# Time mixing: the place of the modulation sums and of the gate's product in the slots

## The chip, the cores and the metric

The kernel runs on one core of one Trainium2 chip. The metric is the device time of one launch in microseconds (us), as the median of several runs.

## The reference

One sequence of 256 tokens with 2048 features goes through two layers. The first is RWKV-7 time mixing with a squared-ReLU MLP, the second chunked band attention with such an MLP. The change lies in the first layer's time mixing. Ahead of everything stand the adaLN modulations, vectors that are products of the condition `c` with large matrices:

```python
mod = c @ w_ada[layer] + b_ada[layer]                 # 2048 x 12288 per layer
sh1, sc1, gt1, sh2, sc2, gt2 = jnp.split(mod, 6, axis=-1)
h = modulate(rms_norm(x, g_mix[layer]), sh1, sc1)
...
r, k, v = xr @ w_r, xk @ w_k, xv @ w_v                # time mixing
g = jax.nn.sigmoid(xg @ g1) @ g2                      # the gate
def step(S, inp):                                     # per head of 64, over 256 tokens
    sa = jnp.einsum('bhvk,bhk->bhv', S, -kk_t)
    S = S * w_t[:, :, None, :] + sa[..., None] * (kk_t * a_t)[:, :, None, :] + v_t[..., None] * k_t[:, :, None, :]
    y = jnp.einsum('bhvk,bhk->bhv', S, r_t)
...                                                   # group norm of y, bonus term
y = y.reshape(B, T, D) * g
return y @ w_o
```

## The kernel before

All activations are kept transposed, with 128 features on the partitions and 256 tokens along the free axis. Matrices are read as float32, split into a high and a low part (ScalarE casts the high part `wH`, L424; VectorE subtracts, `wL`, L427) and multiplied in three passes (L447 to L449, the "projection").

**Slots.** Time mixing treats the 2048 features as 16 pairs of heads (class `Pair`). Each pair is cut into 36 steps: 8 early ones, 12 that invert a triangular matrix, and 16 late ones, which run the recurrence over four chunks, normalise and multiply by the gate. A loop over slots in `layer_a` advances every live pair by one step; a new pair starts every 8 slots, so four or five pairs are live at once. In slot s, pair j stands at step s - 8(j + 1). Within a slot the steps go in the order of a key: inversions first, then late steps (the oldest pair first), then early steps. The step that sums squares over partitions (the last but two) has the key raised by 2 and so comes last. Behind these small steps stand the slot's parts of the dense projections `k` and `r` of the next pair (after slot 128 parts of the output projection). `tc.issue_after(last)` keeps TensorE (PE) in this order; the order on the other engines is set by the scheduler, from the data that each instruction needs.

**Gate's product.** A pair's last step multiplies the gate's low-rank factor `tg` by its weights `lg` on PE (L369) into a PSUM buffer `ms`, and VectorE multiplies the result into `v` (L371). There are two `ms` buffers, and they serve all small steps: the inversion's last product leaves one of them only when ScalarE has copied it out as `uf` (L292).

**Modulation sums.** In six of eight slots, after the projection, `self.ada()` takes one tile of a modulation matrix and VectorE adds it, weighted with `c`, into one accumulator (`acc`, L503 for the first of 16 tiles, L505 for the others). After the 16th tile the accumulator has to be summed over partitions: `ada_sum` issues 32 narrow matmuls against a column of ones (L527) into an `ms` buffer and adds the bias on VectorE (L531). `ada_sum` is a generator, and `self.fin(n)` advances it:

```python
        if kt == KT - 1:
            self.fins = self.ada_sum(self.acc, self.mods[key], half, self.ada_src(*key)[1])
            if not self.lazy:
                self.fin(HK)
```

`lazy` is False throughout this kernel, so the matmuls follow the 16th tile's accumulation at once. There are six such sums in time mixing. The next tile of a new sum calls `fin` too, ahead of writing the accumulator.

Other names in the rows: `iv`, `tt`, `xs`, `u`, `al` belong to the inversion (L264 is VectorE's transpose `tt`, L281 and L276 are ScalarE's copies `xs`); `lt`, `g`, `sa`, `zs`, `kr`, `vp`, `mk` to the recurrence (L104, L348 for `zs`); L191 to L202 are the early steps' VectorE work, L173 to L185 their scan and ScalarE functions.

Of the kernel before, what the change touches and what calls it, by code (L numbers as in the profile page):

```python
# [30 lines left out]
HK = 8  # L31
# [343 lines left out]
class Body:  # L375
# [332 lines left out]
    def layer_a(self, st, sp):  # L708
        nc, tc, d = self.nc, self.tc, self.d
# [7 lines left out]
        with ExitStack() as s1:  # L717
# [19 lines left out]
            sums = pb.tile([P, 2, KT], F32, name="sums01")  # L737
# [117 lines left out]
            for n in range(KT):  # L855
# [12 lines left out]
                first, last = n == 0, n == KT - 1  # L868
# [45 lines left out]
        with ExitStack() as s1:  # L914
            pw = self.pw = s1.enter_context(tc.tile_pool(name="pw", bufs=1, reuse_waits="tile"))
            pp = self.pp = sp.enter_context(tc.tile_pool(name="ps_b", bufs=1, space=bass.MemoryType.PSUM,
                                                         reuse_waits="tile"))
            self.psm = lambda: pp.tile([P, 512], F32, tag="ms", bufs=2, name="ms")
            self.bones = pw.tile([P, P], F32R, name="bones")
            nc.scalar.copy(self.bones, self.cst("bones"))  # L920
            e01 = [pw.tile([P, 4, C + 1], F32, name=f"e01_{i}") for i in range(2)]
            self.uf = [pw.tile([P, 4, C], F32, name=f"uf_{i}") for i in range(2)]
            for e, u in zip(e01, self.uf):
                nc.vector.memset(e[:, :, 0:1], 1.0)
                nc.gpsimd.memset(u, 0.0)

            s1.enter_context(self.ada_room(3))
            self.ada_left = self.ADA_A
            pairs = [Pair(self, j, v[:, j, :], tw, ta, tg, e01[j % 2]) for j in range(NPAIR)]

            def proj_steps(pr):
                for dst, hl in (("k", xk), ("r", xr)):
                    ps = pp.tile([P, 2 * T], F32, tag="pj", bufs=1, name="pj")[:, :T]
                    for kt in range(KT):
                        if kt % HK == 0:
                            w = [self.w_made.popleft()] * (KT // HK)
                        self.proj(ps, w, lambda kt: hl[:, kt, :, 0:T], (kt, kt + 1))
                        if dst == "r" and kt == 1:
                            pr.lw = pw.tile([P, 2, P], F32, tag="lw", bufs=1, name="lw")
                            nc.sync.dma_start(out=pr.lw, in_=d["lora2"][pr.j, :, 0:2])  # L940
                        if kt % 2 == 1:
                            if kt == KT - 1:
                                t = pw.tile([P, T], F32, tag=dst, bufs=2, name=dst)
                                nc.scalar.copy(t, ps)  # L944
                                setattr(pr, dst, t)
                            yield

            def out_steps():

                for n in range(8):  # L950
                    self.split(self.y_hl, n, v[:, n, :])
                sums, todo = self.o_ps, [(n, 0, HK) for n in range(8)] + [(n, HK, KT - 2) for n in range(4)]
                for n, lo, hi in todo:
                    if n % 2 == 0 and lo == 0:
                        if n != 6:
                            tag, k = {0: ("pj", 1), 2: ("iv", 1), 4: ("gr", 2)}[n]
                            ps = pp.tile([P, k, 2 * T], F32, tag=tag, bufs=1, name="o")
                            sums += [ps[:, i].rearrange("p (i t) -> p i t", i=2) for i in range(k)]
                    if lo == HK and n == 0:
                        assert all(p.done for p in pairs[:KT - 2])  # L960
                        for j in range(HK, KT - 2):
                            self.split(self.y_hl, j, v[:, j, :])
                    w = self.weight_part(d["w_o"][n], lo, hi)
                    for kt in range(lo, hi, 2):
                        self.proj(sums[n // 2][:, n % 2, :], w, lambda kt: self.y_hl[:, kt, :, 0:T],
                                  (kt, kt + 2), n % 2 == 0, False)
                        yield

            self.o_ps = []
            S, OUTS = self.SLOTS, 44  # L970
            inverts = range(Pair.EARLY, Pair.EARLY + Pair.INVERT)
            outs, done, n_out = None, 0, 0
            for slot in range(S * NPAIR + Pair.STEPS):
                live = []
                for j, pr in enumerate(pairs):
                    at = slot - S * (j + 1)
                    if 0 <= at < Pair.STEPS:
                        if at == 0:
                            pr.gen = pr.steps()
                        sums = at == Pair.STEPS - 3  # L980
                        live.append((0 if at in inverts else 1 + (at < Pair.EARLY) + 2 * sums, -at, pr))
                        pr.done = at == Pair.STEPS - 1
                last = self.last_pe()
                for _, _, pr in sorted(live, key=lambda x: x[:2]):
                    with tc.issue_after(last):
                        next(pr.gen)
                    last = self.last_pe()
                if slot < S * NPAIR:
                    if slot % S == 0:
                        dense = proj_steps(pairs[slot // S])  # L990
                    todo = 16 // S
                else:
                    if outs is None:
                        self.y_hl = self.new_hl()
                        outs = dense = out_steps()
                    todo = OUTS * (slot + 1 - S * NPAIR) // Pair.STEPS - n_out
                    n_out += todo
                with tc.issue_after(last):
                    for _ in range(todo):
                        next(dense, None)  # L1000
                if slot == 2 * S - 4:
                    self.ada_fill()
                with self.behind():
                    if slot % S in (1, 3, 6, 7):
                        self.w_make()
                    if slot >= 2 * S and slot % S in (0, 1, 2, 4, 6, 7):
                        self.ada()
            self.ada_drain(3)
            self.ada_left = -1
            self.fin(HK)  # L1010
        return v

    def out_proj(self, pp, wname, hl, gate, g, sc, sh, begun=()):
# [310 lines left out]
```

## Time and profile before

| | |
|---|---|
| median of 3 runs | 2648.93 us (2644.81 to 2649.68) |
| the profiled execution | 2651.01 us, of which the span is 2649.2 us |
| PE busy | 2558.2 us, 97% of the span |
| mean granted clock of TensorE | 0.987 |
| time mixing's slots | about 217 to 700 us of the span |

The span reaches from the first to the last instruction of one profiled execution; its own time is 1.8 us more. Rows of a timeline give start, duration, engine, line, operation, output<-inputs, shapes and count, and in brackets how long the engine sat idle before and what released it. PEld is the load of TensorE's weights; a granted clock of 1.00 is full speed.

### The profile page before, as it was taken

Reading aid. Unit: us, or ns where it says so; the run is one execution under the profiler, and the core shown is the slowest. Engines: PE = TensorE matmul, PEld = TensorE weight load, DVE = VectorE, ACT = ScalarE, POOL = GpSimd, SP = SyncE. Lnnn points to the kernel's source line nnn. Section 1 sums busy time; section 2 is a strip of 40 time slices with the busy share of each in tenths; the row PEclk is TensorE's granted clock in tenths of the full one; section 3 lists DMA queues with packets and bytes.
Section 4 is the critical chain, followed back from the end, with each engine's and each line's share of the span. In section 5 each row is a group of like instructions: output and inputs, shape, how many; then the busy total and the mean of one; then the engine's idle time right before and its main releaser. Section 6 shows DMA issues by size and latency. Waiting matters only on the chain.

```text
span 2649.2 us, 58856 instructions
## 1 busy us (share of the span) xinstructions
PE 2558.2 (97%) x23980; PEld 2236.9 (84%) x23980; DVE 2084.7 (79%) x3022; ACT 1372.3 (52%) x2532; POOL 215.4 (8%) x338
## 2 busy tenths in 40 slices
PE   7998999999999999999999999999999999999997
PEld 4788888887899888888888998887898888888886
DVE  6887888888889888888888898899897555555555
ACT  3346566565455355354365554565564464453554
POOL 1002323232100000000001000000100000000002
PEclk9999999998999999999999999999999999999999
DMA  9975666565778889889898679887766555555553
GB/s 351 322 260 189 203 206 204 191 218 173 255 236 300 326 324 328 326 320 341 326 329 288 230 255 326 305 288 259 259 219 235 186 190 187 188 190 188 187 189 121
DMA packets 207664, 663.17 MB, mean 250 GB/s; under 512 B 21409, under 2 KB 55073, under 8 KB 207393
## 3 DMA queue, kind: packets, MB, share of 16 engines
q1 hardware_dynamic: 205328, 656.89, 72.2%
q8 instruction: 188, 3.08, 0.5%
q10 hardware_dynamic: 2064, 2.53, 0.3%
q14 instruction: 84, 0.68, 0.1%
HBM read 657.23 MB, written 2.10 MB: 249 GB/s over the span
## 4 chain that ended last, share of the span: by engine, by line
PE 72%; DVE 1%; DMA 0%; issue 0%; ACT 0%; DVEq 0%; SPq 0%; ACTq 0%
PE pj L458 43%; PE pj L460 21%; PE pj L448 2%; PE pj L447 2%; PE pj L449 2%; PE pT L1212 0%; PE m L527 0%; PE po L1219 0%; PE S L1191 0%; PE S L1190 0%; DMA rada<-w_ada 0%; DVE wL L427 0%; DVE acc L505 0%; PE po L1220 0%; PE o L448 0%
## 5 line engine op out<-in xcount | busy, mean ns | idle before, releaser
L427 DVE TENSOR_TENSOR wL<-raw,wH 128x1024 fp32r<-128x1024 f32 x772 | 946.2, 1227 | 350.1 <-ACT wH L424 348.0
L424 ACT CAST wH<-raw 128x1024 fp32r<-128x1024 f32 x772 | 806.0, 1045 | 741.9 <-PE pj L458 584.8
L458 PE MATMUL pj<-aHL,wH 128*128 128x512 f32 x2816 | 893.6, 398 | 2.6 <-DVE x L1037 1.7
L458 PE MATMUL pj<-hHL,wH 128*128 128x512 f32 x2048 | 644.2, 396 | 0.0
L460 PEld LDWEIGHTS pj<-aHL,wL 128*128 128x128 f32 x2816 | 531.5, 189 | 123.7 <-issue 0.3
L460 PE MATMUL pj<-aHL,wL 128*128 128x256 f32 x2816 | 563.1, 281 | 0.0
L505 DVE SCALAR_TENSOR_TENSOR acc<-rada,ct,acc 128x1024 f32<-128x1024 f32 x360 | 466.4, 1296 | 11.2 <-DMA rada<-w_ada 10.7
L460 PEld LDWEIGHTS pj<-hHL,wL 128*128 128x128 f32 x2048 | 384.2, 188 | 90.7 <-DVE wL L427 0.2
L458 PEld LDWEIGHTS pj<-aHL,wH 128*128 128x128 f32 x2816 | 431.7, 189 | 10.6 <-issue 9.0
L460 PE MATMUL pj<-hHL,wL 128*128 128x256 f32 x2048 | 402.0, 278 | 0.0
L458 PEld LDWEIGHTS pj<-hHL,wH 128*128 128x128 f32 x2048 | 312.0, 189 | 1.3 <-DVE hHL L1083 1.1
L447 PE MATMUL pj<-aHL,wH 128*128 128x256 f32 (+1 forms) x896 | 263.6, 294 | 4.7 <-ACT k L944 4.3
L448 PE MATMUL pj<-aHL,wH 128*128 128x256 f32 (+1 forms) x896 | 254.9, 285 | 0.0
L449 PE MATMUL pj<-aHL,wL 128*128 128x256 f32 (+1 forms) x896 | 253.6, 283 | 0.0
L592 POOL TENSOR_TENSOR ss<-ss,sq 128x256 f32<-128x256 f32 x56 | 50.7, 906 | 1589.4 <-ACT sq L591 1551.3
L447 PEld LDWEIGHTS pj<-aHL,wH 128*128 128x128 f32 x896 | 170.8, 191 | 10.3 <-ACT k L944 5.0
L1108 DVE SCALAR_TENSOR_TENSOR x<-pj,mod,x 128x256 f32<-128x256 f32 x256 | 123.2, 481 | 64.1 <-PE pj L460 61.1
L449 PEld LDWEIGHTS pj<-aHL,wL 128*128 128x128 f32 x896 | 171.2, 191 | 0.2
L448 PEld LDWEIGHTS pj<-aHL,wH 128*128 128x128 f32 x896 | 170.8, 191 | 0.4
L1080 ACT ACTIVATE t<-t 128x256 f32<-128x256 f32 x112 | 46.8, 418 | 120.0 <-DVE t L1052 120.0
L1083 DVE TENSOR_TENSOR hHL<-t,hHL 128x256 fp32r<-128x256 f32 x128 | 53.7, 420 | 1.6 <-ACT t L1082 0.8
L1082 ACT ACTIVATE t<-t 128x256 f32<-128x256 f32 x128 | 53.3, 416 | 3.3
(255 smaller groups left out, 2743.0 us busy)
## 6 DMA issues: line engine op xcount, KB each, us to landing
rada<-w_ada SPq DMA_DIRECT2D x320, 512.0 KB, 5.2
raw<-w_up SPq DMA_DIRECT2D x256, 512.0 KB, 4.3
raw<-w_down SPq DMA_DIRECT2D x256, 512.0 KB, 4.3
rada<-w_ada_kv SPq DMA_DIRECT2D x64, 512.0 KB, 5.9
rawa<-w_ada SPq DMA_DIRECT2D x32, 512.0 KB, 6.8
rawa<-w_ada_t SPq DMA_DIRECT2D x32, 512.0 KB, 7.1
raw<-w_k SPq DMA_DIRECT2D x32, 512.0 KB, 3.6
raw<-w_r SPq DMA_DIRECT2D x32, 512.0 KB, 4.9
```

Source lines behind the costliest of these rows:

```text
L424: nc.scalar.copy(Hf, raw)
L427: eng.tensor_tensor(out=Lf, in0=raw, in1=Hf, op=ALU.subtract)
L447: nc.tensor.matmul(ps, H[:, i, :], a(kt)[:, 0, :], start=(first and kt == 0), stop=False)
L448: nc.tensor.matmul(ps, H[:, i, :], a(kt)[:, 1, :], start=False, stop=False)
L449: ins = nc.tensor.matmul(ps, L[:, i, :], a(kt)[:, 0, :], start=False, stop=(last and kt == KT - 1))
L458: nc.tensor.matmul(ps, w[kt // HK][0][:, kt % HK, :], a(kt), start=(kt == 0), stop=False)
L460: ins = nc.tensor.matmul(ps[:, 0, :], w[kt // HK][1][:, kt % HK, :], a(kt)[:, 0, :], start=False, stop=(kt == KT - 1))
L505: nc.vector.scalar_tensor_tensor(out=self.acc, in0=raw, scalar=ck, in1=self.acc, op0=ALU.mult, op1=ALU.add)
L592: (eng or nc.gpsimd).tensor_tensor(out=self.ss, in0=self.ss, in1=sq, op=ALU.add)
L1082: nc.scalar.activation(t, t, AF.Square)
L1083: nc.vector.tensor_tensor(out=h[:, 1, :], in0=t, in1=h[:, 0, :], op=ALU.subtract)
L1108: nc.vector.scalar_tensor_tensor(out=x, in0=ps[:, i, :], scalar=self.mods[(layer, 5)][:, n:n + 1], in1=x, op0=ALU.mult, op1=ALU.add)
```

## The change

Two things move, and no instruction is added or taken away. `lazy` is set during the loop over slots, so a sum is not issued behind the tile that completes it but in the following slot, after that slot's small steps and ahead of its projection. And the last step of a pair, the gate's product, gets the raised key, so that it comes behind all other small steps of its slot.

```diff
@@ -970,6 +970,7 @@
             outs, done, n_out = None, 0, 0
+            self.lazy = True
             for slot in range(S * NPAIR + Pair.STEPS):
@@ -977,7 +978,7 @@
                             pr.gen = pr.steps()
-                        sums = at == Pair.STEPS - 3
+                        sums = at in (Pair.STEPS - 3, Pair.STEPS - 1)
                         live.append((0 if at in inverts else 1 + (at < Pair.EARLY) + 2 * sums, -at, pr))
@@ -985,6 +986,9 @@
                         next(pr.gen)
                     last = self.last_pe()
+                with tc.issue_after(last):
+                    self.fin(HK)
+                last = self.last_pe()
                 if slot < S * NPAIR:
@@ -1008,6 +1012,7 @@
             self.fin(HK)
+            self.lazy = False
         return v
```

The first place is TensorE around the second sum (rows with `pj` are the projection; those between are the next slot's small steps).

```order
 L448 MATMUL pj<-aHL,wH 128x256
 L449 MATMUL pj<-aHL,wL 128x256
-L527 MATMUL ms<-csts,acc 32x1 x32
 L135 MATMUL ms<-tt,co 32x32 x8
 L135 MATMUL iv<-tt,al 32x32 x16
 L104 MATMUL lt<-zs,kr 64x64 x2
 L140 MATMUL ms<-sq,bones 128x256 x2
+L527 MATMUL ms<-csts,acc 32x1 x32
 L447 MATMUL pj<-aHL,wH 128x256
 L448 MATMUL pj<-aHL,wH 128x256
```

The sum stood directly behind the projection and now stands behind four groups of small steps.

The second place is the slot of a pair's last step. On TensorE (the small steps of four pairs, then the projection):

```order
 L135 MATMUL ms<-u,xs 32x32 x8
 L135 MATMUL iv<-u,xs 32x32 x16
-L369 MATMUL ms<-tg,lg 128x256 x2
 L104 MATMUL lt<-vp,mk 64x64 x2
 L104 MATMUL lt<-kr,zs 64x64 x2
 L104 MATMUL lt<-g,uf_2159 64x64 x2
+L369 MATMUL ms<-tg,lg 128x256 x2
 L447 MATMUL pj<-aHL,wH 128x256
 L448 MATMUL pj<-aHL,wH 128x256
```

The gate's product goes behind the late step of another pair. On ScalarE in the same slot, before:

```order
L177 ACTIVATE s<-s 128x256
L292 COPY uf_2160<-ms 32x4x32 x2
L183 ACTIVATE s<-s 128x256
L336 ACTIVATE sa<-lt 128x64
L184 ACTIVATE s<-s 128x256
L424 CAST wH<-raw 128x1024
L185 ACTIVATE s<-s 128x256
```

And after, on ScalarE in that slot:

```order
L177 ACTIVATE s<-s 128x256
L292 COPY uf_2160<-ms 32x4x32 x2
L336 ACTIVATE sa<-lt 128x64
L424 CAST wH<-raw 128x1024
L183 ACTIVATE s<-s 128x256
L184 ACTIVATE s<-s 128x256
L185 ACTIVATE s<-s 128x256
```

The late step's copy `sa` and the cast of the next weights go ahead of the early step's three functions.

The third place is VectorE from that slot to two slots later, before (without the first rows of the slot):

```order
L371 TENSOR_TENSOR v<-ms,sl 128x256
L200 TENSOR_TENSOR kr<-r,e_1_2158 128x4x64
L427 TENSOR_TENSOR wL<-raw,wH 128x1024
L348 SCALAR_TENSOR_TENSOR zs<-lt,pc,zd 128x64
L191 SCALAR_TENSOR_TENSOR s<-s 128x256
L195 SCALAR_TENSOR_TENSOR s<-s,k 128x256
L192 SCALAR_TENSOR_TENSOR s<-s 128x256
L505 SCALAR_TENSOR_TENSOR acc<-rada,ct,acc 128x1024
L194 SCALAR_TENSOR_TENSOR s<-k,vecs,s 128x256
L287 TENSOR_TENSOR u<-u,iv 128x128
L297 TENSOR_TENSOR mk<-gr,csts 128x512
L264 STREAM_TRANSPOSE tt<-u 128x128
```

And after, on VectorE from the gate's product on:

```order
L371 TENSOR_TENSOR v<-ms,sl 128x256
L427 TENSOR_TENSOR wL<-raw,wH 128x1024
L191 SCALAR_TENSOR_TENSOR s<-s 128x256
L195 SCALAR_TENSOR_TENSOR s<-s,k 128x256
L348 SCALAR_TENSOR_TENSOR zs<-lt,pc,zd 128x64
L192 SCALAR_TENSOR_TENSOR s<-s 128x256
L505 SCALAR_TENSOR_TENSOR acc<-rada,ct,acc 128x1024
L194 SCALAR_TENSOR_TENSOR s<-k,vecs,s 128x256
L287 TENSOR_TENSOR u<-u,iv 128x128
L198 TENSOR_TENSOR kr<-s,e_1_2158 128x4x64
L264 STREAM_TRANSPOSE tt<-u 128x128
```

`zs` goes behind L191 and L195, and the transpose `tt` stands behind `kr` (L198), no longer behind `mk` (L297), which follows it.

## The prediction

> **What bounds the kernel now.** I read the page first, then the waits of TensorE (PE), then the granted clock by stretches, then the timeline of one head pair. The page says that PE is the bound:
>
> ```profile
> PE 2558.2 (97%) x23980; PEld 2236.9 (84%) x23980; DVE 2084.7 (79%) x3022; ACT 1372.3 (52%) x2532; POOL 215.4 (8%) x338
> ```
>
> So only time in which PE waits, or runs at a lower clock, can be won. The change touches the slots of time mixing alone, roughly 290 to 664 us of the span. The waits of PE there (engine, what waits, for whom; total us, times, longest):
>
> ```profile
> PE ms L527 <- DVE acc L505: 9.4, 5, 2.6
> PE ms L369 <- ACT uf L292: 8.8, 11, 1.0
> PE ms L135 <- ACT xs L281: 2.5, 1, 2.5
> PE iv L135 <- DVE tt L264: 2.4, 8, 0.3
> ```
>
> The first row is the modulation sums, the second the gate's product: the two things that are moved. The third is a small step that waits for ScalarE's copy L281, the fourth one that waits for VectorE's transpose; both stand in the slots between. Now the same stage by stretches, cut where the clock changes (start:end, us, PE busy, granted clock, DMA share, GB/s):
>
> ```profile
> 240.30:243.70 3.40, 2.01 (x49) 1.00 0.90 293
> 291.40:294.90 3.50, 1.66 (x27) 1.00 0.63 225
> 294.90:298.30 3.40, 3.40 (x128) 0.57 0.54 159
> 366.60:370.00 3.40, 1.93 (x119) 1.00 0.73 196
> 370.00:376.80 6.80, 6.08 (x77) 0.54 0.40 138
> 513.40:516.80 3.40, 1.93 (x24) 1.00 0.46 157
> 516.80:523.60 6.80, 6.64 (x174) 0.53 0.25 80
> 588.40:591.90 3.50, 0.96 (x41) 1.00 0.66 235
> 591.90:595.30 3.40, 3.40 (x111) 0.57 0.82 233
> 290.00:664.00 374.00, 345.28 (x8113) 0.95 0.61 196
> ```
>
> After each stretch of 3.4 us in which PE was busy for 0.96 to 1.93 us the clock was about half for 3.4 or 6.8 us; after 2.01 us (first row) it was not. The sums' own waits lie in or next to those gaps:
>
> ```profile
> 294.76 0.71 PE L527 MATMUL ms<-csts,acc 128*32 128x1 f32 x64 [1.84 <-DVE acc L505]
> 368.07 0.70 PE L527 MATMUL ms<-csts,acc 128*32 128x1 f32 x64 [2.57 <-DVE acc L505]
> 516.96 0.87 PE L527 MATMUL ms<-csts,acc 128*32 128x1 f32 x64 [1.63 <-DVE acc L505]
> 591.62 0.70 PE L527 MATMUL ms<-csts,acc 128*32 128x1 f32 x64 [2.54 <-DVE acc L505]
> 663.43 0.70 PE L527 MATMUL ms<-csts,acc 128*32 128x1 f32 x64 [0.84 <-DVE acc L505]
> ```
>
> Four of the five are followed by a slow stretch. A sum thus costs its wait and then half a clock.
>
> **Sums one slot later.** No instruction is added or removed. Each of the six sums goes behind the next slot's small steps, whose inputs stand ahead of the last accumulation in VectorE's order. PE then works in the time in which it waited. What is inserted, by the rows of such slots:
>
> ```profile
> 434.44 0.45 PE L135 MATMUL iv<-u,xs 32*32 32x32 f32 x32
> ...
> 435.64 0.38 PE L447 MATMUL pj<-aHL,wH 128*128 128x256 f32 x1
> ...
> 368.70 0.34 PE L135 MATMUL ms<-tt,co 32*32 32x32 f32 x10
> 369.61 0.50 PE L140 MATMUL ms<-sq,bones 128*128 128x256 f32 x2
> ...
> 664.06 0.45 PE L135 MATMUL ms<-tt,al 32*32 32x32 f32 x32
> 664.72 0.28 PE L104 MATMUL lt<-g,uf 64*64 64x64 f32 x4
> ```
>
> First and fourth sum: 435.64 - 434.44 = 1.20 us, so 1.84 and 1.63 become 0.64 and 0.43. Second and fifth: from 368.70 to 369.61 + 0.50 = 370.11, 1.41 us, so 2.57 and 2.54 become 1.16 and 1.13. The last: from 664.06 to 665.00, 0.94 us against 0.84, nothing left. The third sum shows no wait. Left are 3.4 of 9.4 us: **6.0 us won**. The bounds are 9.4 won, if VectorE comes earlier too, and 6.0 - 2 x 2.5 = 1.0, for a wait that is new: two of the sums (second and fifth) now take a PSUM buffer that the copy L281 has to free, and the longest wait for that copy was 2.5. In the new order L281 stands ahead of the exponential L175, so I take 6.0. Queued behind a sum are the slot's projection on PE and, on VectorE, the modulation add L531 and the next start of the accumulator, L503. In the new order these two stand behind other small steps of the later slot and at least one row behind where PE issues the sum, so I count nothing for them. On SyncE one load of lora rows and one of an ada tile change places with a neighbour, twice in the stage; GpSimd's order is the same. That costs nothing, as no wait of PE names either load.
>
> **The clock.** The slow stretches cost 3.40 x 0.43 = 1.46 us, 6.08 x 0.46 = 2.80, 6.64 x 0.47 = 3.12 and 1.46 again (PE's busy time in them times the clock that is missing): 8.8 us. The largest wait left is 1.16 us of a 3.4 us stretch, so PE would be busy for over 2.0 of it, on the side of the row that kept its clock, if narrowly. Bounds: 0 if the clock falls all the same, 8.8 if it never does. I take **8.8**.
>
> [...]
>
> **The gate's product.** One pair, slot 3 of 8 (the page's names; uf, L292, is the copy that frees the PSUM buffer that the product takes):
>
> ```profile
> 427.96 0.51 ACT L292 COPY uf<-ms 32x128 f32<-32x128 f32 x2
> 428.52 1.13 PE L369 MATMUL ms<-tg,lg 128*128 128x256 f32 x4 [0.98 <-ACT uf L292]
> 429.58 0.33 PE L104 MATMUL lt<-vp,mk 64*64 64x64 f32 x4
> 430.08 0.38 PE L447 MATMUL pj<-aHL,wH 128*128 128x256 f32 x1
> ...
> 430.93 1.03 ACT L424 CAST wH<-raw 128x1024 fp32r<-128x1024 f32 x1
> 432.00 1.23 DVE L427 TENSOR_TENSOR wL<-raw,wH 128x1024 fp32r<-128x1024 f32 x1 [1.31 <-ACT wH L424]
> ...
> 433.14 0.28 DVE L348 SCALAR_TENSOR_TENSOR zs<-lt,pc,zd 128x64 f32<-128x64 f32 x1
> 433.33 0.42 DVE L191 SCALAR_TENSOR_TENSOR s<-s 128x256 f32<-128x256 f32 x1
> 433.67 0.42 DVE L195 SCALAR_TENSOR_TENSOR s<-s,k 128x256 f32<-128x256 f32 x1
> ...
> 435.33 0.22 PE L104 MATMUL lt<-zs,kr 64*64 64x64 f32 x2
> 436.60 0.68 DVE L297 TENSOR_TENSOR mk<-gr,csts 128x512 f32<-128x512 f32 x1
> 437.43 0.37 DVE L198 TENSOR_TENSOR kr<-s,e 128x256 f32<-128x256 f32 x1
> 437.64 0.45 PE L135 MATMUL iv<-tt,al 32*32 32x32 f32 x32 [0.31 <-DVE tt L264]
> ```
>
> The order shows that the product still takes the buffer of uf, so it cannot start before 428.5. But the late step's matmuls, 430.08 - 429.58 = 0.50 us, now run inside the wait. Eight waits of about 0.98 (7.8 of the 8.8 us) give 0.50 each, 4.0; the three short ones, 1.0 together, are below 0.50 each and go: **5.0 us won**, between 4.0 and the whole 8.8.
>
> ScalarE now casts the next weights (L424) ahead of the three steps that wait for VectorE, so that the 1.31 us in which VectorE sat before L427 goes. The three come up to 1.03 us later for it, which L191 bears, behind that same L427 (1.23). In slot 5 the transpose tt stands behind kr (0.37) and no longer behind mk (0.68): 0.31 us earlier, as much as PE waits for it. PE comes 0.50 earlier too, and VectorE's 1.31 covers that. So the 2.4 us of the third row go, between 0 and 2.4; I take **2.4**. If the 1.31 stays, tt is late again.
>
> **Given back.** After the second and fifth sum the product found its buffer free, because PE was slow; in time again, it waits 0.48 there: **-1.0 us**. Sum: 6.0 + 8.8 + 5.0 + 2.4 - 1.0 = 21.2 us. The profiled execution took 2651.0, so 2629.8. It stood 2.1 us above the median of the three runs, 2648.9, whose own spread is 4.9; I don't take that off and say **2630**. Below about 0.2%, 5.3 us, such a run can't be told from no change.
>
> **The rivals.** *The clock falls all the same*, by the short waits together or for a cause of its own. Then 8.8 is lost and the 1.0 isn't given back: 12.2 + 1.0 = 13.4 us won, 2638. For it speaks how close 1.16 us of waiting comes to the row with 2.01 busy; against it, that the long gaps all end in a sum. [...]
>
> *Nothing is gained*: the small steps ahead of a sum wait for VectorE as the sum did, and the product's wait moves with its buffer. Against it stand the 1.31 us that VectorE waits in each pair, so it isn't what holds the stage. About 2647.
>
> *Slower: zs comes late.* On VectorE L371, which waits for the product, stands ahead of the weights and zs, and L191 and L195 come before zs too. Now zs is done at 433.42 and used at 435.33, 1.9 us of slack; 0.84 for the two and 0.50 for PE's gain leave 0.57. A held-up L371 looked like this in a slow stretch:
>
> ```profile
> 626.94 0.42 DVE L371 TENSOR_TENSOR v<-ms,sl 128x256 f32<-128x256 f32 x1 [1.42 <-PE ms L369]
> ```
>
> With 1.42 in every pair zs would be 0.85 late in each of 16 pairs, 13.6 us; with a slow stretch of 1.46 each, 23.4 more: 37 - 21.2 = 16 us lost, 2667. It decides from 0.57 us of such holding up in each pair, if the 1.31 stays; if that goes, as I think, it never comes.
>
> **How the numbers follow.** The forecast 0.58, the falling clock 0.22, nothing gained 0.12, slower 0.08. Faster is the first two, 0.80; same 0.12; slower 0.08. All that can be won is 9.4 + 8.8 + 8.8 + 2.4 = 29.4, to 2622: the lower end. The upper end, 2643, takes in the falling clock with a few waits more, to where 2 in 10 lie above. The forecast's own range is 2622 to 2637.
>
> **What would show it.** Sums: waits of L527 at 0.4 to 1.2 us, one slot later, and no clock below 1.00 behind them; with the clock low there, the clock term was wrong. Gate: L369 waits about 0.5 in most pairs. L427 without its 1.31, the wait on tt gone. If waits on zs or sq appear on PE in their place, the inserted steps were no cover.

## The result: about 22 us faster, and the profile after

Six runs of the changed kernel took 2626.85 us in the median (2624.38 to 2635.01), six of the kernel before beside them 2649.30: a ratio of 0.9915, with a 95% interval of 0.9902 to 0.9928. A second comparison, below, gave 2631.06 us and 0.9927. The predicted 2630 lies between them. The profiled execution after took 2624.4 us, against 2651.0 before.

The waits of PE in the slots of time mixing after the change (290 to 664 us; engine, what waits, for whom; total, times, longest):

```profile
PE ms L369 <- ACT uf L292: 3.5, 8, 0.5
...
PE ms L527 <- DVE acc L505: 1.6, 2, 0.9
PE ms L140 <- ACT sl L363: 1.5, 6, 0.5
PE ms L135 <- DVE tt L264: 1.2, 2, 0.6
PE ms L527 <- ACT g L329: 0.9, 1, 0.9
...
PE iv L135 <- DVE tt L264: 0.4, 1, 0.4
```

The gate's product waits 3.5 us in place of 8.8, the sums 1.6 + 0.9 in place of 9.4, the inversion's step on `tt` 0.4 in place of 2.4. Two rows have grown: the sums of squares L140 now wait 1.5 us (0.4 before) until ScalarE (L363) has read the PSUM buffer that their result takes, and two other steps of the inversion wait 1.2 us together (0.3 before) for `tt`, at 597 and 611 us.

The first five sums, one slot later each (the sixth, at 639.15 us, waits for nothing either):

```profile
296.33 0.71 PE L527 MATMUL ms<-csts,acc 128*32 128x1 f32 x64 [0.68 <-DVE acc L505]
364.92 0.70 PE L527 MATMUL ms<-csts,acc 128*32 128x1 f32 x64 [0.93 <-ACT g L329]
436.64 0.82 PE L527 MATMUL ms<-csts,acc 128*32 128x1 f32 x64
503.38 0.71 PE L527 MATMUL ms<-csts,acc 128*32 128x1 f32 x64
572.72 0.70 PE L527 MATMUL ms<-csts,acc 128*32 128x1 f32 x64 [0.93 <-DVE acc L505]
```

The slot of a pair's last step, on PE, PE's weight loads, ScalarE and VectorE:

```profile
419.53 0.51 ACT L292 COPY uf<-ms 32x128 f32<-32x128 f32 x2
420.09 1.13 PE L369 MATMUL ms<-tg,lg 128*128 128x256 f32 x4 [0.46 <-ACT uf L292]
420.85 0.19 PEld L447 LDWEIGHTS pj<-aHL,wH 128*128 128x128 f32 x1
...
421.76 1.21 DVE L427 TENSOR_TENSOR wL<-raw,wH 128x1024 fp32r<-128x1024 f32 x1
423.69 0.29 DVE L348 SCALAR_TENSOR_TENSOR zs<-lt,pc,zd 128x64 f32<-128x64 f32 x1
426.20 0.22 PE L104 MATMUL lt<-zs,kr 64*64 64x64 f32 x2
428.13 0.45 PE L135 MATMUL iv<-tt,al 32*32 32x32 f32 x32
```

The product waits half as long; L427 follows without its 1.31 us, and no wait on `tt` stands at the last row. `zs` ends 2.2 us before it is used. The granted clock (start:end, us, PE busy, clock, DMA share, GB/s), after:

```profile
290.00:600.00 310.00, 298.40 (x7214) 1.00 0.67 215
596.52:599.93 3.41, 1.14 (x53) 1.00 0.69 264
599.93:603.34 3.41, 3.41 (x68) 0.50 0.73 208
```

From 290 to 600 us the kernel before had four stretches at half clock, 20.4 us in all. After, the first comes at 599.9 us, behind no sum.

The four stretches before begin at 295.40, 370.50, 517.27 and 592.36 us and last 3.41, 6.83, 6.83 and 3.41 us. Their starts lie 75.10, 146.77 and 75.09 us apart, which is 22, 43 and 22 times 3.413. After, stretches at half clock begin at 599.93, 617.00 and 678.44 us, which is 5 and 18 times. Stretches of the clock are therefore cut here in steps of 3.413 us, counted from where half clock begins or ends in the same trace. Cut so, the stretches of one or two steps shown here have a clock of 1.00 or 0.50; the cuts in the prediction lie about 0.5 us off, and its slow rows show 0.53 to 0.57.

To find where the time came from I use one interval that holds the first five sums and eleven of the gate's products: from the projection's wait for ScalarE's `k` (291 to 293 us) to the gate's product that follows the fifth sum. Its ends before, then after:

```profile
291.22 0.39 PE L447 MATMUL pj<-aHL,wH 128*128 128x256 f32 x1 [0.35 <-ACT k L944]
597.00 1.13 PE L369 MATMUL ms<-tg,lg 128*128 128x256 f32 x4
```

```profile
292.79 0.38 PE L447 MATMUL pj<-aHL,wH 128*128 128x256 f32 x1 [0.35 <-ACT k L944]
576.11 1.13 PE L369 MATMUL ms<-tg,lg 128*128 128x256 f32 x4
```

It took 305.8 us before and 283.3 after: 22.5 us, as much as the difference between the medians. The other 4 us between the two profiled executions lie outside it. Each interval is of one execution, and two traces of the same kernel differ in it by 2.3 and 2.6 us (table below).

### The profile page after: what moved, and what is told of

It is laid out like the page before. It is cut to its first block, busy times and chain, and to the rows that moved or that the text cites. A ratio compares the mean times of both kernels' runs of the same rounds, so it can differ in the third digit from the quotient of the medians.

```text
span 2622.6 us, 58848 instructions
## 1 busy us (share of the span) xinstructions
PE 2547.0 (97%) x23980; PEld 2230.0 (85%) x23980; DVE 2082.6 (79%) x3022; ACT 1376.6 (52%) x2532; POOL 220.2 (8%) x338
## 4 chain that ended last, share of the span: by engine, by line
PE 72%; DVE 1%; DMA 1%; ACT 0%; issue 0%; DVEq 0%; ACTq 0%; SPq 0%
PE pj L458 42%; PE pj L460 21%; PE pj L448 2%; PE pj L447 2%; PE pj L449 2%; DMA rada<-w_ada 0%; PE pT L1217 0%; PE m L527 0%; PE po L1224 0%; DVE acc L505 0%; DVE wL L427 0%; PE S L1196 0%; DMA raw<-w_q 0%; PE S L1195 0%; PE po L1225 0%
## 5 line engine op out<-in xcount | busy, mean ns | idle before, releaser
L427 DVE TENSOR_TENSOR wL<-raw,wH 128x1024 fp32r<-128x1024 f32 x772 | 945.6, 1226 | 338.4 <-ACT wH L424 335.2
L505 DVE SCALAR_TENSOR_TENSOR acc<-rada,ct,acc 128x1024 f32<-128x1024 f32 x360 | 462.5, 1285 | 11.6 <-DMA rada<-w_ada 11.1
L1085 ACT ACTIVATE t<-t 128x256 f32<-128x256 f32 x112 | 46.9, 419 | 119.7 <-DVE t L1057 119.7
L1086 ACT ACTIVATE hHL<-t 128x256 fp32r<-128x256 f32 x128 | 52.9, 414 | 4.1 <-DVE t L640 3.1
```

What stands on the lines that cost most here:

```text
L427: eng.tensor_tensor(out=Lf, in0=raw, in1=Hf, op=ALU.subtract)
L505: nc.vector.scalar_tensor_tensor(out=self.acc, in0=raw, scalar=ck, in1=self.acc, op0=ALU.mult, op1=ALU.add)
L1086: nc.scalar.activation(h[:, 0, :], t, AF.Square)
```

## The experiments

"Interval" is the one above, in each kernel's own trace. "Half clock" is the time at half clock from 290 to 600 us there. Ratios are to the kernel before, timed on the same chip.

| kernel | median, us | ratio, 95% interval | interval, us | half clock, us |
|---|---|---|---|---|
| before | 2649 to 2652 | 1 | 305.8 | 20.4 |
| the change | 2626.85 | 0.9915 [0.9902, 0.9928] | 283.3 | 0 |
| the change again | 2631.06 | 0.9927 [0.9914, 0.9941] | 285.9 | 3.4 |
| sums alone | 2640.91 | 0.9966 [0.9953, 0.9978] | 295.0 | 3.4 |
| gate's product alone | 2636.68 | 0.9956 [0.9943, 0.9969] | 291.6 | 13.6 |
| before, gaps filled | 2643.19 | 0.9975 [0.9964, 0.9987] | 299.5 | 3.4 |
| before, one filler each | 2647.63 (one run; 2647.15 for before, beside it) | – | 302.2 | 10.2 |
| gate alone, gaps filled | 2634.81 | 0.9943 [0.9930, 0.9955] | 290.0 | 3.4 |
| change + own bank | 2625.00 | 0.9906 [0.9892, 0.9919] | 282.6 | 3.4 |
| the same again | 2624.28 | 0.9900 [0.9883, 0.9917] | 280.3 | 3.4 |
| change + own bank for both | 2625.75 | 0.9909 [0.9896, 0.9923] | 285.5 | 13.6 |
| change + own bank, filled | 2624.85 | 0.9900 [0.9883, 0.9917] | 283.8 | 3.4 |
| before, narrow fillers | 2681.73 | 1.0113 [1.0096, 1.0130] | – | 37.5 |
| before, small fillers | 2647.23 | 0.9986 [0.9972, 1.0001] | 304.2 | 13.6 |

### Which half brings what

Sums alone:

```diff
-                        sums = at in (Pair.STEPS - 3, Pair.STEPS - 1)
+                        sums = at == Pair.STEPS - 3
```

> Only the modulation sums move behind the next slot's small steps; the gate's product keeps its old place. My theory (a sum costs its wait and then half a clock): the five waits on the accumulator fall from 9.4 to about 3 us, no stretch of low clock follows a sum (8.8 us back), and an ordinary pair keeps its period of 26.6 us: about 14 us faster, ratio near 0.9947. Rival (the clock falls for causes of its own): the waits fall in the same way, slow stretches of the same total length stay, about 6 us faster, ratio near 0.9977.

Gate's product alone (the kernel before with the new key):

```diff
-                        sums = at == Pair.STEPS - 3
+                        sums = at in (Pair.STEPS - 3, Pair.STEPS - 1)
```

> Only the gate's product moves behind the other small steps; the sums stay directly behind the projection. My theory: the period of an ordinary pair falls from 26.6 to about 25.6 us, as in the changed kernel; the sums keep waits of 1.6 to 2.6 us or a little more (TensorE reaches them earlier) and the slow stretches behind them: about 7 to 9 us faster, ratio near 0.997. Rival (the period fell because the sums no longer disturb the other engines): the period stays at 26.6 and the time within 2 us of before.

Measured were 8.9 us for the sums, between the two expectations (the interval of the ratio holds the rival's 0.9977 and not the theory's 0.9947), and 13.1 for the gate's product, well above the 7 to 9 expected. The sums alone still had one stretch at half clock, behind the fifth sum, which waited 0.94 us. In the interval the halves brought 10.8 and 14.2, together 25.0 against 22.5 for both: the two overlap. The waits of the gate's half alone, and its fourth and fifth sum, show one place where they do:

```profile
PE ms L527 <- DVE acc L505: 8.6, 5, 2.6
PE ms L369 <- ACT uf L292: 3.8, 8, 0.5
...
505.72 0.71 PE L527 MATMUL ms<-csts,acc 128*32 128x1 f32 x64 [0.61 <-DVE acc L505]
...
576.06 0.70 PE L527 MATMUL ms<-csts,acc 128*32 128x1 f32 x64 [2.60 <-DVE acc L505]
```

The fourth sum, still in its old place, waits 0.61 us instead of 1.63, and no half clock follows. With the 1.31 us on L427 gone, VectorE comes to that accumulation earlier. Without the sums' move, the first, second and fifth wait as before and the clock falls behind each. In the sums alone the waits of L369 (8.7 us) and on `tt` (2.4) stayed.

### The clock by itself

The kernel before, with matmuls in the gaps whose result nobody reads, and nothing moved. Three, four, three and four stand ahead of the first, second, fourth and fifth sum. The lines shift by four: L531 is the sum, L528 the filler (`x6` are three fillers).

```diff
+        for _ in range({0: 3, 1: 4, 3: 3, 4: 4}.get(self.n_sum, 0)):
+            nc.tensor.matmul(full[:, 256:512], self.cst("ones"), self.csts[:, 0:256], start=True, stop=True)
```

> The order of before, but ahead of the first, second, fourth and fifth sum TensorE gets 3, 4, 3 and 4 extra 128x128 by 128x256 matmuls that depend on nothing and whose result nobody reads (about 0.5 us each, so they fill 1.6 or 2.1 us of the wait). The sums start when they started, so no wait is saved; TensorE is only busy in it. My theory: the four slow stretches behind the sums are gone, 7 to 9 us faster, ratio near 0.997. [...]

The ratio came out as expected, and 17 of the 20.4 us at half clock went. Two of its sums:

```profile
292.06 1.46 PE L528 MATMUL ms<-csts 128*128 128x256 f32 x6
294.08 0.71 PE L531 MATMUL ms<-csts,acc 128*32 128x1 f32 x64 [0.56 <-DVE acc L505]
363.36 1.89 PE L528 MATMUL ms<-csts 128*128 128x256 f32 x8
366.00 0.71 PE L531 MATMUL ms<-csts,acc 128*32 128x1 f32 x64 [0.74 <-DVE acc L505]
...
290.00:600.00 310.00, 293.34 (x6879) 0.99 0.63 203
```

The sums still wait for the same accumulations, only that most of the waiting is filled; the waits of L369 (8.6 us) and on `tt` stayed. With most of the gaps of 1.63 to 2.57 us filled, no half clock followed three of the four sums: there the idle gap ahead of the sum was what brought the clock down. With three of the four stretches gone the interval is 6.3 us shorter, where the prediction's rows said 7.4 for these three. This refutes the rival by which the clock falls all the same, though it still fell behind the fifth sum, after a wait of 0.74 us.

What a gap must be was asked with one filler at each of the four:

```diff
-        for _ in range({0: 3, 1: 4, 3: 3, 4: 4}.get(self.n_sum, 0)):
+        for _ in range({0: 1, 1: 1, 3: 1, 4: 1}.get(self.n_sum, 0)):
```

> The kernel before, with only one matmul that nobody reads ahead of each of the first, second, fourth and fifth sum. The waits become about 1.4, 2.1, 1.2 and 2.1 us. Theory: a single wait of up to about 1.45 us in a 3.4 us stretch leaves PE busy for 2.0 of it, and that keeps the clock. So no slow stretch behind the first and fourth sum, one behind the second and fifth. Rival 1: any matmul in the gap is enough, none is slow. Rival 2: what matters is the number of waits close by, not the length of one; then all four are slow as before.

The waits were 1.42, 2.04, 1.21 and 2.04 us. The clock fell behind the second sum and no other. Behind the fifth, with the same wait and PE busy for only 1.97 us of a stretch, it did not, so none of the three expectations held in full. It also fell at 445.5 us, behind a gap of 1.49 us that has no releaser, 3.5 us behind the third sum, which waits for nothing:

```profile
445.09 0.32 PE L104 MATMUL lt<-g,uf 64*64 64x64 f32 x2 [1.49 <-issue]
...
585.43:588.84 3.41, 1.97 (x15) 1.00 0.65 232
588.84:592.25 3.41, 2.81 (x126) 1.00 0.82 274
```

Does it matter which matmuls fill a gap? Two kernels put other fillers into the gaps of the kernel before. The first took narrow ones of the sum's own shape, 120 or 164 in a gap:

```diff
+        for i in range({0: 120, 1: 164, 3: 120, 4: 164}.get(self.n_sum, 0)):
+            g = 32 * (i % 4)
+            nc.tensor.matmul(full[g:g + 32, 256:257], self.csts[:, g:g + 32], self.col(C_ONE),
+                             start=True, stop=True, tile_position=(0, g))
```

> The kernel before, with narrow matmuls that nobody reads (32 columns of weights, one moving column, like the sum's own) in the gaps ahead of the first, second, fourth and fifth sum: 120, 164, 120 and 164 of them, about 11 ns each by the sum's row (64 in 0.70 us), so that 0.5 to 0.8 us of waiting is left, as with the wide ones. [...]

It says nothing on the clock, for two reasons. Each of these matmuls is two of 10 ns in the trace (the sum's 64 rows are 32 matmuls), which the expectation did not reckon with, so 120 of them take some 2.4 us and not 1.3, more than the wait of 1.84 us. And PE stood still in the middle of them, for no releaser; the kernel lost 30 us:

```profile
292.06 0.98 PE L529 MATMUL ms<-csts 128*32 128x1 f32 x97
294.20 0.99 PE L529 MATMUL ms<-csts 128*32 128x1 f32 x61 [1.16 <-issue]
299.57 0.34 PE L529 MATMUL ms<-csts 128*32 128x1 f32 x12 [3.49 <-issue]
```

The second took as many fillers as the wide ones, on 32 rows and 32 columns:

```diff
-            nc.tensor.matmul(full[:, 256:512], self.cst("ones"), self.csts[:, 0:256], start=True, stop=True)
+            nc.tensor.matmul(full[0:32, 256:512], self.cst("ones")[0:32, 0:32], self.csts[0:32, 0:256],
+                             start=True, stop=True, tile_position=(0, 0))
```

> The kernel before, with three, four, three and four matmuls that nobody reads ahead of the first, second, fourth and fifth sum, as in the one with wide matmuls and with as many moving columns (256), but on 32 rows and 32 columns of the array in place of 128 and 128. They take the same time on PE, so 0.3 to 0.75 us of each wait is left. [...]

It came out between the kernel before and the one with wide fillers: the clock fell behind the second and fifth sum, not behind the first and fourth, and the interval of the ratio, 0.9972 to 1.0001, holds both 1 and the 0.9975 of the wide fillers. A third fall, at 444.1 us, comes with a gap of 1.97 us without a releaser, behind the third sum. The stretches around the second sum are worth seeing. First with the small fillers (the sum waits 0.60 us, from 365.04), then with the wide ones (0.74 us, from 365.26):

```profile
363.14 1.91 PE L528 MATMUL ms<-csts 32*32 32x256 f32 x8
...
362.17:365.58 3.41, 2.88 (x17) 1.00 0.42 150
365.58:372.41 6.83, 6.77 (x179) 0.50 0.66 211
```

```profile
362.01:365.43 3.42, 3.25 (x21) 1.00 0.40 137
365.43:368.84 3.41, 2.84 (x127) 1.00 0.88 287
```

After a stretch with PE busy for 2.88 us, most of it with small matmuls, the clock was half for the next 6.8. With wide fillers it stayed after 2.84 us. So the busy time of a step alone does not tell here whether half clock follows. That the kind of matmul makes the difference is not shown: the first and fourth sum kept their clock with the small ones, and with the wide ones the clock fell behind the fifth sum, after 2.67 us.

### What the sums are worth without the clock

The gate's product moved and the sums left in place, with wide fillers ahead of the first, second and fifth (the key as above; `{0: 3, 1: 4, 4: 4}` in the filler's loop):

> The kernel before, with the gate's product moved and the sums left where they were; three, four and four matmuls that nobody reads stand ahead of the first, second and fifth sum (the fourth lost its slow stretch with the gate's move alone). Theory A: moving the sums is worth the clock and little else. From the trace of the gate's move alone 1.46 + 1.46 + 3.1 us of slow clock go: from the stage's first marker to the gate's product of the fifth sum's pair 285.6 us (the changed kernel took 283.3), ratio 0.9930. Theory B, the prediction's: the waits themselves are worth what their rows say, 7.7 us less the 2.5 that are left, and the extra matmuls fill them for nothing; then it takes 288.5 there, 5 us more than the changed kernel, ratio 0.9937.

The interval was 290.0 us with one stretch of 3.4 us left at half clock (1.7 us of PE's time), so 288.3 without it: nearer theory B's 288.5 than A's 285.6. The whole kernel's ratio, 0.9943, lies nearer B's too, though its interval holds both, and single traces differ by 2.3 to 2.6 us. The changed kernel timed beside it (the change again, with one such stretch too) was 4.1 us shorter in the interval and 3.8 in the median. So the waits of the sums are worth something beside the clock; that it is all that their rows say is likely and not shown.

What the clock brought here is less clear. The interval is only 1.6 us shorter than with the gate's move alone, though 7.7 us less of it run at half clock (11.1 to 3.4), about 3.6 us of PE's time; the ratios of the two, 0.9943 and 0.9956, differ by 3.4 us.

### What is left after the change

The change once more, and with the gate's product in the pair's own PSUM bank:

> The changed kernel once more, beside the kernels below. 2626 to 2627 us, ratio 0.9915 as in the first comparison. In the trace: no slow stretch between 290 and 590 us, as before. If the slow stretches of the stage's last third (610 to 700 us) lie elsewhere or last otherwise than in the first trace of it, what was saved there (about 7 us of slow clock) belongs to the single execution and not to the change.

```diff
-            pg = b.psm()[:, :T]
+            pg = bank[:, 0, :]
```

> The changed kernel, with the gate's product written into the pair's own PSUM bank instead of one of the two shared buffers. Theory: what is left of the gate's wait (3.5 us, eight times 0.46) is the wait for that buffer alone. Then it goes, and the kernel is 3 to 4 us faster than the changed one: ratio to the kernel before 0.990. The 1.5 us by which the variance sums L140 wait for the reader of their buffer stay or grow. Rival: the product is no bound there, VectorE's transposes and zs come late when PE is 0.46 us earlier in each pair; then waits on tt or zs appear in place of it and the ratio stays at 0.9915.

The change again was slower than the first time, though within the spread of such comparisons, and it had a stretch at half clock behind the fifth sum, at 573.9 us, behind a wait of 0.94. From 600 to 720 us its trace had 20.4 us at half clock, as many as the kernel before, where the first trace after had 10.2: what seemed saved there belongs to the single execution.

With its own bank, the product waits for nothing. Its starts in successive pairs:

```profile
316.20 1.13 PE L369 MATMUL lt<-tg,lg 128*128 128x256 f32 x4
341.26 1.13 PE L369 MATMUL lt<-tg,lg 128*128 128x256 f32 x4
368.20 1.13 PE L369 MATMUL lt<-tg,lg 128*128 128x256 f32 x4
```

An ordinary pair (the first two starts; a sum lies between the other two) takes 25.06 us, where the change took 25.60 and the kernel before 26.62. The 0.5 is the wait that the change had left. The interval is 3.3 us shorter than in the change again, as expected; the median was 6 us lower than its neighbour's and 2 lower than the first time, so the size of the gain is between these. Run again:

> The changed kernel with the gate's product in the pair's own bank once more, beside the one with the extra matmuls: 2625 us, ratio 0.9906. A slow stretch behind the second or the fifth sum in this trace too would bear out that a wait of 0.93 us brings the clock down about every second time; none leaves it as it is.

It was 2624.28 us and 0.9900, with no half clock behind a sum (the one of 3.4 us began at 596.6). Its interval is 3.0 us shorter than that of the change's first trace, which had none behind a sum either.

The variance sums in that bank too:

```diff
-        var = b.psm()[:, :T]
+        var = bank[:, 0, :]
```

> As the one with the product in the pair's own bank, and the variance sums (second group of L140) in that bank too, so that neither takes a shared buffer. Theory: the 1.5 us by which L140 waits for ScalarE's function L363 go as well; 5 us faster than the changed kernel, ratio 0.9895, 2622. Rival: as above, waits on VectorE's results take their place; ratio 0.9915.

The time is that of the bank for the product alone, as the rival said. The wait for L363 went, and other waits stand in the trace, on VectorE's `tt` and on GpSimd's `al`:

```profile
PE ms L135 <- DVE tt L264: 2.0, 3, 1.3
PE gr L104 <- issue: 1.9, 1, 1.9
PE ms L135 <- POOL al L257: 1.6, 2, 0.9
```

They need not have taken its place: the second trace of the product's bank alone has the rows on `tt` and `al` too, at 1.6 and 1.5 us. The clock also fell behind both the second and the fifth sum in this trace (waits of 0.93), with 13.6 us at half clock where the product's bank alone had 3.4. Why nothing was gained stays open. Last, the own bank with two wide fillers ahead of each of these two sums (`{1: 2, 4: 2}` in the loop):

> The changed kernel with the gate's product in the pair's own PSUM bank, and two matmuls that nobody reads ahead of the second and of the fifth sum, where it waits 0.93 us. So far the clock fell behind one of these two sums in about half of the traces in which they waited 0.74 to 0.94 us, and behind the first and fourth, which waited 0.68 or less, never. Theory: it is the wait that brings it down; with two matmuls of 0.45 us in it nothing is left, and no slow stretch comes between 290 and 600 us. Ratio to the kernel before 0.9895 to 0.990, 1.5 to 3 us faster than without the matmuls. [...]

The time did not change, though no half clock followed the two sums. The first filler of each waited itself, 0.41 us for `xs`, since the sum's buffer is what it writes into. And the clock fell elsewhere, 5 us behind the fourth sum, in a gap without a releaser:

```profile
507.24 0.34 PE L104 MATMUL gr<-csts,v 64*64 64x64 f32 x7 [1.46 <-issue]
...
504.54:507.95 3.41, 1.95 (x71) 1.00 0.23 59
507.95:511.36 3.41, 3.41 (x65) 0.50 0.81 269
```

## Why the prediction was right, and where its steps were off

**Sums one slot later: held.** Predicted were waits of 0.64, 1.16, 0, 0.43, 1.13 and 0 us, 3.4 in all; measured were 0.68, 0.93, 0, 0, 0.93 and 0, 2.5 in all. The fourth is lower because VectorE comes earlier by the gate's move, the bound that the prediction had named and not taken. As time, the gain shows best between kernels that lost the same half clock. The sums alone and the kernel before with its gaps filled both keep the stretch behind the fifth sum: 299.5 less 295.0 is 4.5 us. The gate alone with its gaps filled and the change again have one each: 290.0 less 285.9 is 4.1. The prediction's four sums there make 5.2.

**The clock: the gaps cost it, but the prediction's criterion did not hold.** That the gaps ahead of the sums cost clock is shown by the wide fillers, with which 17 of the 20.4 us at half clock went. In the first trace after the change no half clock was left behind a sum. But the step that said PE busy for over 2.0 of 3.4 us keeps the clock is wrong. It was read from stretches that were cut about 0.5 us too early. Cut in steps of 3.413 us, the kernel before already speaks against it; its second sum waits from 365.50 to 368.07 us:

```profile
363.67:367.08 3.41, 1.84 (x14) 1.00 0.46 177
367.08:370.50 3.42, 2.43 (x123) 1.00 0.86 246
```

The clock stayed after 1.84 us and fell, at 370.50, after 2.43. The cost came out too small for the same reason: in those steps PE is busy for 19.8 us at half clock, which makes 9.9 us and not 8.8, and 8.2 and not 7.4 for the three stretches that the wide fillers took away, of which the interval gave back 6.3.

After waits of 1.6 us and more it fell 8 times of 9 in these traces (four sums before, three with the gate alone, two of 2.04 us). Behind the sums that waited 0.94 us or less it fell in 7 of 16 cases at the second and fifth and in none of 17 at the first and fourth (wide fillers counted, small and narrow ones not; nor the fillers on top of the own bank). In 6 of the 16 cases the end of a step of 3.413 us cuts the wait in two, with about 0.1 us or more on either side, and the clock fell in none of them; in the other 10 it fell in 7. In the first trace after, for one, 599.93 us less 69 and 8 steps is 364.41 and 572.62, in the waits that end at 364.92 and 572.72. This was counted afterwards and not tested. The prediction took the whole 8.8 for certain; with 7 of 16 at two sums, about 0.9 stretches of 3.4 or 6.8 us come back in each execution, 1.7 to 3.4 us each. That is an estimate from these counts.

**The gate's product: right in kind, mis-sized.** The period of an ordinary pair fell by 1.02 us, from 26.62 to 25.60. Predicted were 0.50 for the work inside the wait and 0.31 for `tt`. The wait went from 0.98 to about 0.47, as said, and `tt` came in time. What was missed stands in a row of the kernel before:

```profile
429.58 0.19 PEld L104 LDWEIGHTS lt<-vp,mk 64*64 64x64 f32 x4 [0.33 <-issue]
```

The late step's weight loads, in their old place right behind the product, began 0.33 us late, and the projection's load came 3.03 us after the loads of the inversion's step (427.05 to 430.08). Ten of the eleven pairs up to 600 us have that gap of 0.33 us. Behind the moved product the projection's load follows without such a gap, and the same distance is 2.20 us (418.65 to 420.85): 0.83 us less. The first matmul of the projection then takes 0.47 us instead of 0.38, so that from its second one on (430.30 and 421.18) 0.72 us are left, not 0.50. In the slot of `tt` the matmuls come 0.39 us sooner (from one projection to the next 2.07 us before, 1.68 after), not 0.31. In the slot of L140 they come about 0.05 us later (1.74 and 1.79). Together that is the 1.02 to 1.06 us of an ordinary pair. Over the eleven products of the interval, 1.02 each is 11.2 us; the trace of the gate's move alone shows 9.8 (14.2 less 1.0 of the fourth sum's wait and 3.4 of its clock). The prediction had 5.0 + 2.4 - 1.0 = 6.4 for all.

**VectorE: held.** Its waits on `wH` ahead of L427, in the same 374 us, before and after:

```profile
DVE wL L427 <- ACT wH L424: 14.3, 11, 1.4
```

```profile
DVE wL L427 <- ACT wH L424: 2.4, 2, 1.4
```

**Given back: wrong.** The product was to wait 0.48 us again behind the second and fifth sum. It doesn't (368.29 and 576.11 us, no wait). The copy `uf` ends at 368.17 and 575.98 us, ahead of it. The sum's own 0.70 us and its wait of 0.93 stand 3.4 us ahead of the product and may be what delays PE; this reading was not tested.

**Missed: new waits.** L140 waits 1.5 us for the reader of its buffer, 1.1 more than before, and two steps of the inversion 1.2 us together for `tt`, 0.9 more, outside the interval.

**The rivals.** That the clock falls all the same is refuted by the fillers, as an account of why it falls; it does fall now and then. That nothing is gained is refuted. That `zs` comes late: it keeps 2.2 us, more than the 1.9 before, because the 1.31 us of VectorE went.

In sum: the prediction's terms make 5.2 + 8.8 + 6.4 = 20.4 us in the interval, and its two traces show 22.5 and 19.9. The terms as measured one by one are 4.1 to 4.5 for the sums, 6.3 for the first three slow stretches and up to 1.7 for the last, and 9.8 to 11.2 for the gate's product: 20 to 24 us, which fits the whole within the 2.6 us between traces. The halves alone make more, 25.0; one reason is that each of them saves the fourth sum's clock. So the total came right with a gate term that was too small by some 4 us and a clock term and a sums term that were too large by some 1 to 2.5 and by 1. That these cancel is luck.

## What to carry to other kernels

A short wait of the matmul engine cost more than its length here where half clock followed it (1.63 us ahead of the fourth sum, and 3.4 us of lost clock behind it): look at the granted clock behind each wait, in stretches cut where the clock changes, and test the suspicion with matmuls that nobody reads in the gap before anything is moved. When a product waits for a shared buffer, put other work into the wait (26.62 to 25.60 us a pair here) or, better here, give it a bank of its own (25.06). Then time the next buffer in line before you move it too: here, removing that wait as well brought nothing (2625.75 us against 2625.00). A gain at an engine that isn't the bound (VectorE's 1.31 us) turned up here at places that were priced separately, so the halves of the change, 10.8 and 14.2 us, don't add up to its 22.5.

## What the runs showed of the hardware that was not expected

- The stretches at half clock in time mixing began whole multiples of 3.413 us apart (22, 43 and 22 times in the kernel before, from 295.40 us on; 5 and 18 times after, from 599.93 us on). After a wait of 0.74 to 0.94 us ahead of the second or fifth sum the clock fell in 7 of 10 cases where the wait lay within one such step, and in none of 6 where a step's end cut it; why was not tested.
- Half clock came once after a step of 3.41 us in which the profile has PE busy for 2.88 us, most of it with matmuls on 32 rows and 32 columns (second sum, small fillers). With 128 rows and columns in the same place the clock stayed at 1.00 after 2.84 (wide fillers).
- Gaps of 1.3 to 2.0 us for which the profile has no releaser come 3 to 5.5 us behind the third or fourth sum in seven of the traces. Half clock came with three of them (1.46, 1.49 and 1.97 us) and not with the other four (1.30 to 1.69). They come at different places in different traces; a part of the spread between runs may lie there, which was not tested.
- Behind rows of matmuls of 10 ns (97 in 0.98 us in the narrow fillers) PE stood idle for 0.4 to 3.5 us without a releaser, and the kernel with 568 such matmuls more (1136 in the trace) lost 30 us, with the half clock that followed them. Whether the gaps behind the sums, of 64 such matmuls each, are of the same kind is open.
- Weight loads of 64x64 behind a 128x128 product began 0.33 us late, in ten of eleven pairs; a 128x128 load in that place did not.
